# Three gate and shift vectors of a transformer block as column-tiled products on TensorE

## The chip, the cores and the metric

The kernel runs on one core of a Trainium2 chip. The metric is the device time of one execution in microseconds (us), here the median of three runs. Next to it stands one execution that the hardware profiler recorded; the rows of this document come from that one.

## The reference, cut to what matters

One block of a diffusion transformer in fp32, width 2048, with 256 latent tokens `x` and 256 context tokens `ctx`. The vector `c` gives six modulation vectors; what concerns this change is the first line:

```python
mods = jnp.split(jax.nn.silu(c) @ ada_w[l] + ada_b[l], 6, axis=-1)      # ada_w: 2048 x 12288
sh_m, sc_m, gt_m, sh_f, sc_f, gt_f = (m[:, None, :] for m in mods)      # numbers 0 to 5
h_lat = modulate(x_lat, norm_mix_pre[l], sh_m, sc_m)
mix_ctx, mix_lat = token_mixer(h_ctx, h_lat, rows, w_in[l], ...)        # S5, gated delta, mLSTM
x_lat = x_lat + gt_m * rms_norm(mix_lat @ w_out[l], norm_mix_post[l])
f_lat = swiglu(modulate(x_lat, norm_ffn_pre[l], sh_f, sc_f), ffn_w_gate[l], ffn_w_up[l], ffn_w_down[l])
x_lat = x_lat + gt_f * rms_norm(f_lat, norm_ffn_post[l])
```

Modulations 0 and 1 (`sh_m`, `sc_m`) are needed at once, for both token sets. Modulation 2 (`gt_m`) is needed after the mixer, 3 and 4 (`sh_f`, `sc_f`) before the feed-forward layer, 5 (`gt_f`) at the very end. Each is a product of one row of 2048 numbers with a 2048 x 2048 weight block of 16 MB.

## The kernel before

**The big products.** Every large product splits an fp32 weight tile `wf` (512 KB, 1024 columns in each of 128 partitions) into a high part `wh` (ScalarE, `copy`, L168) and a low part `wl = wf - wh` (`tt`, L157, on VectorE or GpSimd), and TensorE adds up three products (`mm3`, tiles `s`). `Unit` is one such tile and `Feed` a list of them that runs through the whole kernel: `Feed.ahead` loads and splits tiles ahead, `Feed.pull(us)` emits so many microseconds of their matmuls. The generators of the stages (`s5`, `gates`, `mlstm`, `prep`, `inv`, `outputs`) yield estimates of time, and `run` pulls as much of the feed between two of their steps. `feed.lo` says which low parts go to GpSimd: 0 none, n each n-th.

**The stages**, with their places in the profiled execution: modulations 0 and 1 as raw tiles `ada` together with the S5 tables (to about 150 us); S5 (150 to 420 us, of it the scan at 217 to 275 us and the part with tables `cf` on GpSimd and products `k` and `y` on TensorE at 276 to 393 us); gates and mLSTM (to 563 us); the gated delta heads (563 to 1010 us, the input weights are used up at 800 us); output product and second norm (to 1072 us); gate and up products (to 1548 us); down product.

**Modulations 2 to 5 in `Modulation`.** A step of `step_` takes one weight tile `vw` of 128 rows by 512 columns (256 KB) and adds it, times one number per partition, to the accumulator `vacc` on VectorE: `ts` (L164) for the first and `stt` (L160) for the other 15 of a block. After 16 steps `finish` sums over the partitions with four matmuls against `ones` (tile `vm`). `Modulation.pull` is called from `Feed.pull`; `rate` sets how many steps are emitted for a microsecond of feed. Modulations 3, 4 and 2 (192 steps) run beside the stages from S5 on, 5 (64 steps) beside the feed-forward products. `load` keeps three tiles in flight.

**What sets the order.** Each engine and each DMA queue works its instructions in order. The order is the emission order as rearranged by the Tile scheduler, which hoists what is ready; nearly all loads stand in one queue, SyncE's (`dma`, L136). `behind(i, first)` adds an ordering without a wait on hardware. In `Modulation.load` the first three loads of modulation 5 are held back by a ScalarE write that needs the last tile of the second norm; those of modulation 3 are not held back at all. The matmuls outside the feed share four PSUM banks `m` (`bank`).

Of the kernel before, what the change touches and what calls it, by code (L numbers as in the profile page):

```python
# [19 lines left out]
P = 128  # L20
# [61 lines left out]
def body(tc, ins, out):  # L82
# [34 lines left out]
    with es:  # L117
# [61 lines left out]
        DVE.memset(mhalf, -0.5)  # L179
        ones = ctile([P, P], "ones")  # L180
# [31 lines left out]
        class Unit:  # L212
# [69 lines left out]
        class Feed:  # L282


            def __init__(self):
                self.units, self.i, self.nl, self.ns = [], 0, 0, 0
                self.gen, self.posts, self.credit, self.done = None, [], 0.0, set()
                self.side, self.open, self.over = None, set(), set()
                self.first, self.lo = {}, 0
# [262 lines left out]

        with pool("st") as st, pool("st2", 2) as st2, pool("aw") as aw, pool("xr") as xr:
# [22 lines left out]
            DVE.memset(csz, 0.0)  # L576
            act(cs32, c32, AF.Tanh, scale=0.5)
# [4 lines left out]
            DVE.tensor_copy(cT.rearrange("p s k -> p (s k)"), ps[:, 0:32])  # L582
            DVE.tensor_copy(csz[:, :, 0:2], cT.rearrange("p s k -> p k s"))
# [205 lines left out]
            def ada_units(b):  # L789
# [4 lines left out]
                for part in range(2):  # L794
                    c0 = (1 - part) * D + b * 512
                    for kp in range(8):
# [8 lines left out]
                        def post(part=part):  # L805
# [18 lines left out]
                            for kk in range(5):  # L824
# [7 lines left out]
                                if kk:  # L832
# [5 lines left out]
                                      aw, 9))  # L838
# [61 lines left out]
        class Modulation:  # L900
# [68 lines left out]

            def move(self, vp):  # L970

                self.end = -(-self.nl // NK) * NK
# [3 lines left out]
        kms, qms, vas = {}, [], []  # L976

        def k_ev(j, ps):
            kms[j] = hold(f"km{j}")
            copy(kms[j], ps)  # L980

        def q_ev(j, ps):
            if j == 0:
                qm = hold("qm")
                qms.extend(qm[:, S * i:S * i + S] for i in range(3))
            act(qms[j], ps, AF.Copy, scale=0.125)

        def v_ev(h0):
            def f(bs):
                for t, ps in bs:  # L990
                    if not vas:
                        vas.append(hold("va")[:, 0:3096].rearrange("p (t h c) -> p t h c", t=4, c=129))
                        DVE.memset(vas[0][:, :, :, P:P + 1], 1.0)
                    copy(vas[0][:, t, h0:h0 + ps.shape[1] // P, 0:P], ps.rearrange("p (h c) -> p h c", c=P))
                    yield
            return f
# [298 lines left out]
        with pool("s1") as s1, pool("s2", 2) as s2:  # L1295
# [3 lines left out]
            feed.lo, side.rate = 2, 0.3  # L1299
# [265 lines left out]
        feed.lo = 3  # L1565
# [297 lines left out]
        feed.lo = 2  # L1863
# [115 lines left out]
        for n in range(4):  # L1979
            gm.append(wo.tile([P, 512], F32, tag="vw" if n < 3 else "vacc", name="gm", bufs=3 if n < 3 else None))  # L1980
# [130 lines left out]
        feed.side = Modulation((5,), 0.12, v2, h2l[15][:, S - 1:S])  # L2111
# [72 lines left out]
```

## Time and profile before

| | before |
|---|---|
| median of three runs | 1808.94 us (1806.25 to 1809.45) |
| the profiled execution | 1800.1 us |
| its span, first to last instruction | 1798.3 us |
| mean granted TensorE clock | 0.949 |
| instructions | 26078 |

The profile gives for each engine its busy time, and for TensorE apart matmuls (PE) and weight loads (PEld). A stretch of the span can be asked for by itself. An fp32 matmul shows as two records (x16 are 8 matmuls); `128*32` behind MATMUL is the part of the array that is used, `128x256` what comes out. PEclk is the granted clock as a share of full speed.

### The profile page before, as it was taken

How to read it: one execution, taken by the hardware profiler on the slowest of the kernel's cores; microseconds unless marked ns; L12 is line 12 of the kernel's file. 1: busy time of each engine (PE TensorE's matmuls, PEld its weight loads, DVE VectorE, ACT ScalarE, POOL GpSimd, SP SyncE). 2: the span in 40 equal slices, each digit the busy share in tenths (PEclk: the TensorE clock that was granted, in tenths of full speed). 3: DMA queues.
4: the chain of work that ended last, by engine and by line, in shares of the span. 5: the costliest groups of instructions: out<-in, count | busy, mean ns of one | idle time of the engine just before them, and what ended most of it. 6: DMA issues, size and time to landing. Idle time of an engine off the chain costs nothing. (4 is left out here: it accounts for less than half of the span.)

```text
span 1798.3 us, 26078 instructions
## 1 busy us (share of the span) xinstructions
PE 1632.5 (91%) x9732; PEld 1331.3 (74%) x9732; DVE 1112.6 (62%) x1793; ACT 756.9 (42%) x1282; POOL 395.7 (22%) x356
## 2 busy tenths in 40 slices
PE   5897997697899889987899979999999999999998
PEld 2555876575687768776677758888888888888886
DVE  3986495748676788765543587657664455444444
ACT  3324212133445236365455474444444444443443
POOL 1005337831213262144553220000000000000001
PEclk9888897798799899998999979999999999999999
DMA  9995133766746746542222459778776666655553
GB/s 328 361 365 120 57 105 98 225 190 201 236 152 210 228 118 196 175 152 71 81 74 95 152 177 332 248 221 281 213 238 188 188 190 192 208 193 194 192 195 132
DMA packets 209525, 340.46 MB, mean 189 GB/s; under 512 B 24837, under 2 KB 68443, under 8 KB 208503
## 3 DMA queue, kind: packets, MB, share of 16 engines
q1 hardware_dynamic: 202535, 330.06, 57.9%
q0 software_dynamic: 1936, 5.60, 1.1%
q10 hardware_dynamic: 4928, 3.15, 0.6%
q8 instruction: 76, 1.25, 0.3%
q14 instruction: 50, 0.41, 0.1%
HBM read 332.11 MB, written 6.64 MB: 188 GB/s over the span
## 5 line engine op out<-in xcount | busy, mean ns | idle before, releaser
L168 ACT ACTIVATE wh<-wf 128x1024 fp32r<-128x1024 f32 (+1 forms) x404 | 420.7, 1044 | 542.2 <-PE s L108 449.0
L157 DVE TENSOR_TENSOR wl<-wf,wh 128x1024 fp32r<-128x1024 f32 (+1 forms) x349 | 423.7, 1218 | 332.4 <-ACT wh L168 331.4
L108 PE MATMUL s<-wl,h2h 128*128 128x512 f32 x704 | 276.4, 393 | 7.7 <-DVE wl L157 7.7
L108 PE MATMUL s<-wh,h2h 128*128 128x512 f32 x704 | 276.0, 393 | 2.9 <-ACT wh L168 2.9
L108 PE MATMUL s<-wh,h2l 128*128 128x512 f32 x704 | 275.8, 392 | 0.2 <-POOL h2l L157 0.2
L160 DVE SCALAR_TENSOR_TENSOR vacc<-vw,cT,vacc 128x512 f32<-128x512 f32 x240 | 203.0, 846 | 78.4 <-DMA vw<-in_ada_w_dram 75.7
L157 POOL TENSOR_TENSOR wl<-wf,wh 128x1024 fp32r<-128x1024 f32 x55 | 136.0, 2474 | 339.3 <-ACT wh L168 298.0
L108 PE MATMUL s<-hh,wh 128*128 128x512 f32 (+1 forms) x448 | 168.1, 387 | 6.7 <-ACT wh L168 3.6
L108 PE MATMUL s<-hh,wl 128*128 128x512 f32 (+1 forms) x448 | 163.4, 371 | 5.5 <-DVE wl L157 5.3
L157 POOL TENSOR_TENSOR rs<-ss,mhalf 128x1 f32<-128x1 f32 x6 | 3.7, 618 | 743.5 <-ACT ps L168 743.5
L108 PE MATMUL s<-hl,wh 128*128 128x512 f32 (+1 forms) x448 | 165.1, 369 | 0.0
L108 PEld LDWEIGHTS s<-wl,h2h 128*128 128x128 f32 x704 | 133.0, 189 | 37.0 <-DVE wl L157 9.7
L108 PEld LDWEIGHTS s<-wh,h2h 128*128 128x128 f32 x704 | 132.9, 189 | 31.1 <-ACT wh L168 3.9
L108 PEld LDWEIGHTS s<-wh,h2l 128*128 128x128 f32 x704 | 133.0, 189 | 28.0 <-POOL h2l L157 0.6
L108 PE MATMUL s<-wh,ah 128*128 128x512 f32 x352 | 136.8, 390 | 0.0
L108 PE MATMUL s<-wh,al 128*128 128x512 f32 x352 | 136.7, 389 | 0.0
L108 PE MATMUL s<-wl,ah 128*128 128x512 f32 x352 | 136.6, 389 | 0.0
L108 PEld LDWEIGHTS s<-hh,wh 128*128 128x128 f32 x448 | 88.5, 198 | 20.2 <-ACT hh L168 4.1
L108 PEld LDWEIGHTS s<-hh,wl 128*128 128x128 f32 x448 | 88.0, 198 | 20.2 <-DVE wl L157 6.3
L108 PE MATMUL s<-wh,mix 128*128 128x512 f32 x256 | 102.6, 428 | 0.1
L108 PEld LDWEIGHTS s<-hl,wh 128*128 128x128 f32 x448 | 88.6, 198 | 14.1 <-issue 3.1
L108 PE MATMUL s<-wl,hh 128*128 128x256 f32 (+1 forms) x256 | 91.3, 358 | 7.0 <-DVE wl L157 6.3
(626 smaller groups left out, 2746.3 us busy)
## 6 DMA issues: line engine op xcount, KB each, us to landing
vw<-in_ada_w_dram SPq DMA_DIRECT2D x256, 256.0 KB
wf<-in_ffn_w_gate_dram SPq DMA_DIRECT2D x96, 512.0 KB
wf<-in_w_in_dram SPq DMA_DIRECT2D x92, 512.0 KB
wf<-in_ffn_w_up_dram SPq DMA_DIRECT2D x88, 512.0 KB
wf<-in_ffn_w_down_dram SPq DMA_DIRECT2D x88, 512.0 KB
wf<-in_ada_w_dram SPq DMA_DIRECT2D x64, 512.0 KB
wf<-in_w_out_dram SPq DMA_DIRECT2D x32, 512.0 KB
x<-in_x_dram SPq DMA_DIRECT2D x4, 1024.0 KB
```

Of the source, the lines that this page charges most:

```text
L108: return cls.queue(nc.tensor.matmul(*a, **k))
L157: return (eng or DVE).tensor_tensor(out=o, in0=a, in1=b, op=op)
L160: return (eng or DVE).scalar_tensor_tensor(out=o, in0=a, scalar=s, in1=b, op0=op0, op1=op1)
L168: return ACT.activation(out=o, in_=a, func=f, **kw)
```

## The change

A class `Products` takes over modulations 3, 4 and 2; `Modulation` keeps 5. A step of `Products` makes 128 output columns: four loads of 512 rows by 128 columns (again 256 KB each, in pieces of 512 bytes instead of 2 KB), and for each load four fp32 matmuls whose stationary operand is 32 columns wide (column 0 holds numbers of `silu(c)`, `cz`) and which go to four 32-partition groups of one bank `vm`. ScalarE copies the bank to `vrow`, and one step later a matmul with `sel4` adds the four rows and turns the result into a column (`vs`). Per modulation that is 16 steps with 64 loads, 256 matmuls of 32 x 128 and 16 of 128 x 1. `pull` takes four units of credit for a step, so that the bytes per microsecond of feed stay as before.

Besides: the first loads of `Products` and of modulation 5 are ordered behind the last weight load of the feed (`feed.last`) in place of the ScalarE write; the ring of the `ada` tiles goes from 9 to 6 buffers, and the first tile of the keys' product (`mk0`) gets buffers of its own and moves ahead of `feed.need("u")`; `feed.lo` becomes 0 at three places. In numbers of instructions: VectorE loses 180 `stt`, 12 `ts` and 12 sums of `vm` and gains 48 sums of 128 x 1 and 14 `wl`; GpSimd loses 14 `wl`; ScalarE gains 48 copies of 128 x 128; TensorE gains 768 matmuls of 32 x 128 and 48 of 128 x 1 and loses 48 of 128 x 1. The number of DMAs stays.

```diff
-                dma(self.wf, self.src)
+                feed.last = dma(self.wf, self.src)
...
+            cz = ctile([P, 56], "cz")
+            DVE.memset(cz, 0.0)
...
+            DVE.tensor_copy(cz[:, 0:NK], cT[:, 0])
...
-                                      aw, 9))
+                                      aw, 6))
...
             feed.add(uu[6:8])
+            mk = stream_fm("mk0", C_MK, 256, 0, 512, k_ev)
+            mk[0].wf_ring, mk[0].wh_ring, mk[0].tag = [xr], [xr], "mk0a"
+            feed.add(mk)
             run(early_tables())
             feed.need("ada3")
-            feed.need("u")
+            feed.need("u", "mk0a")
...
-                    if self.nl < 3 and self.after is not None:
-                        ACT.activation(out=w[:, 0:1], in_=self.after, func=AF.Copy)
                     c0 = i * D + n * 512
-                    dma(w, ada[k * P:(k + 1) * P, c0:c0 + 512])
+                    behind(dma(w, ada[k * P:(k + 1) * P, c0:c0 + 512]), self.after if self.nl < 3 else None)
...
+        class Products:
...
+            def load(self):
+                while self.nl < 4 * self.end and self.nl < self.used + 3:
+                    (i, n), h = self.todo[self.nl // 4], self.nl % 4
+                    w = self.vp.tile([P, 4, P], F32, tag="vw", name="vw", bufs=3)
+                    c0 = i * D + n * P
+                    behind(dma(w, ada[h * 512:h * 512 + 512, c0:c0 + P].rearrange("(k p) c -> p k c", p=P)),
+                           self.after if self.nl < 3 else None)
...
+            def step(self):
+                PE.fed = True
+                self.load()
+                ps = bank("vm")
+                for h in range(4):
+                    self.load()
+                    w = self.w.pop(self.used)
+                    for k in range(4):
+                        PE.matmul(ps[32 * k:32 * k + 32, 0:P], cz[:, 4 * h + k:4 * h + k + 32], w[:, k],
+                                  start=(h == 0), stop=(h == 3))
+                    self.used += 1
+                self.flush()
+                r = self.vp.tile([P, P], F32, tag="vrow", name="vrow", bufs=2)
+                copy(r, ps[:, 0:P])
...
+            def flush(self):
...
+                ps = bank("vs")
+                PE.matmul(ps[:, 0:1], r, sel4, start=True, stop=True)
...
+            def pull(self, us):
+                self.credit += us * self.rate * 2
+                while self.credit > 0 and self.i < self.end:
+                    self.step()
+                    self.credit -= 4.0
...
-        side = feed.side = Modulation((3, 4, 2), 0.15, vp)
-        feed.add(stream_fm("mk0", C_MK, 256, 0, 512, k_ev))
+        side = feed.side = Products((3, 4, 2), 0.15, vp, feed.last)
...
-            feed.lo, side.rate = 2, 0.3
+            feed.lo, side.rate = 0, 0.3
...
-        feed.lo = 3
+        feed.lo = 0
...
-        feed.lo = 2
+        feed.lo = 0
...
-        feed.side = Modulation((5,), 0.12, v2, h2l[15][:, S - 1:S])
+        feed.side = Modulation((5,), 0.12, v2, feed.last)
```

**SyncE's queue in the first stage** (`wf` from `ada_w` are raw tiles of modulations 0 and 1, `wf` from `w_in` weights of the feed, `vw` tiles of modulation 3). Before:

```order
L136 DMA wf<-in_w_in_dram 128x2x512
L136 DMA wf<-in_ada_w_dram 128x2x512
L136 DMA wf<-in_w_in_dram 128x2x512
L136 DMA vw<-in_ada_w_dram 128x512
L136 DMA wf<-in_ada_w_dram 128x2x512
L136 DMA vw<-in_ada_w_dram 128x512 x2
L136 DMA wf<-in_ada_w_dram 128x2x512 x8
L136 DMA wf<-in_w_in_dram 128x2x512
L136 DMA vw<-in_ada_w_dram 128x512
```

And now:

```order
L136 DMA wf<-in_w_in_dram 128x2x512 x2
L136 DMA wf<-in_w_in_dram 128x4x256
L136 DMA wf<-in_ada_w_dram 128x2x512 x6
L136 DMA wf<-in_w_in_dram 128x2x512 x2
L136 DMA wf<-in_ada_w_dram 128x2x512 x18
L136 DMA wf<-in_w_in_dram 128x2x512
L136 DMA wf<-in_ada_w_dram 128x2x512 x5
```

The `vw` loads are gone from this stage; the tile of 128x4x256 is the first of `mk0`, which stood at the stage's end. The first `vw` load now stands behind the last raw tile.

**TensorE in the S5 part with `k` and `y`** (`s` are the feed's products, `k` and `y` those of the S5 tables). Before:

```order
L108 MATMUL s<-wh,hl_575 128x256
L108 MATMUL k<-cf,bz 32x128 x8
L108 MATMUL s<-wh,hh_570 128x256
L108 MATMUL s<-wl,hh_570 128x256
L108 MATMUL s<-wh,hl_576 128x256
```

And now, in the like place:

```order
L108 MATMUL vs<-sel_80,vrow 128x1
L108 MATMUL k<-cf,bz 32x128 x4
L108 MATMUL s<-wh,hh_579 128x256
L108 MATMUL s<-wl,hh_579 128x256
L108 MATMUL s<-wh,hl_584 128x256
L108 MATMUL vm<-vw,cz 32x128 x4
L108 MATMUL k<-cf,bz 32x128 x2
L108 MATMUL vm<-vw,cz 32x128 x4
L108 MATMUL k<-cf,bz 32x128 x2
L108 MATMUL y<-cf,Sc 32x128 x8
```

The groups of four `vm` matmuls, one for each load, stand among the matmuls of the feed and of the stage, and each group waits for the load of its own tile. In the whole program the 768 form 129 unbroken blocks: 79 of one group of four, 18 of two, 21 of three, and 11 others.

**VectorE in the gated delta heads** (`Y` and `Z` belong to the inversion that the heads wait for, `wl` to the feed). Before:

```order
L157 TENSOR_TENSOR Z<-inv,lv_5552 128x512
L160 SCALAR_TENSOR_TENSOR vacc<-vw,cT,vacc 128x512
L157 TENSOR_TENSOR Z<-inv,lv_5552 128x512
L160 SCALAR_TENSOR_TENSOR vacc<-vw,cT,vacc 128x512 x2
L157 TENSOR_TENSOR Y<-inv,lvc 128x256
L157 TENSOR_TENSOR wl<-wf,wh 128x1024
L160 SCALAR_TENSOR_TENSOR vacc<-vw,cT,vacc 128x512
L157 TENSOR_TENSOR Y<-inv,lvc 128x256
```

And now:

```order
L157 TENSOR_TENSOR wl<-wf,wh 128x1024
L157 TENSOR_TENSOR mod_1554<-vs,cols 128x1
L157 TENSOR_TENSOR Y<-inv,lvc 128x256 x3
L157 TENSOR_TENSOR wl<-wf,wh 128x1024
L157 TENSOR_TENSOR Y<-inv,lvc 128x256 x2
L157 TENSOR_TENSOR wl<-wf,wh 128x1024
```

The sums between the steps of the inversion are gone; a small sum of 128x1 for each 128 columns is left.

## Rows read from the trace of the kernel before

**Rows 1.** Page, part 1: busy us, share of the span, instructions.
```profile
PE 1632.5 (91%) x9732; PEld 1331.3 (74%) x9732; DVE 1112.6 (62%) x1793; ACT 756.9 (42%) x1282; POOL 395.7 (22%) x356
```
**Rows 2.** Busy time by stage: stretch, length, then each engine, PEclk, DMA share, GB/s.
```profile
34.00:130.00 96.00, 85.25 (x644) 56.14 (x643) 91.16 (x244) 31.68 (x57) 8.96 (x5) 0.89 1.01 369
276.00:368.00 92.00, 68.90 (x682) 62.12 (x682) 54.74 (x75) 22.20 (x42) 78.97 (x105) 0.80 0.59 176
393.00:563.00 170.00, 150.62 (x762) 122.75 (x761) 117.98 (x205) 78.52 (x165) 34.19 (x23) 0.91 0.65 201
563.00:800.00 237.00, 215.15 (x1546) 181.69 (x1545) 183.62 (x274) 105.78 (x222) 80.47 (x62) 0.96 0.58 177
1072.00:1548.00 476.00, 475.31 (x2146) 393.61 (x2146) 279.78 (x283) 206.42 (x219) 2.00 (x1) 1.00 0.74 229
```
**Rows 3.** The same by stage for instructions with vacc alone (PE, PEld, DVE).
```profile
34.00:130.00 96.00, 0.00 (x0) 0.00 (x0) 11.62 (x16) 0.89 1.01 369
276.00:393.00 117.00, 4.49 (x24) 4.58 (x24) 42.84 (x48) 0.81 0.61 178
393.00:563.00 170.00, 3.05 (x24) 2.99 (x24) 41.86 (x48) 0.91 0.65 201
563.00:800.00 237.00, 5.69 (x40) 5.90 (x40) 68.85 (x80) 0.96 0.58 177
```
**Rows 4.** Loads of vw from 30 to 130 us; DMA issues of the page, part 6.
```profile
L136 SPq DMA_DIRECT2D vw<-in_ada_w_dram x19: 328/341/653, 34.1 to 122.0; - x19
...
vw<-in_ada_w_dram SPq DMA_DIRECT2D x256, 256.0 KB
```
**Rows 5.** TensorE in order of time: start us, us, engine, instruction, records.
```profile
305.14 0.64 PE L108 MATMUL k<-cf,bz 128*32 128x128 f32 x16
305.72 0.39 PE L108 MATMUL s<-wh,hh 128*128 128x256 f32 x1
...
314.42 0.42 PE L108 MATMUL k<-cf,bz 128*32 128x128 f32 x8
314.77 0.38 PE L108 MATMUL s<-wh,hl 128*128 128x256 f32 x1
```
**Rows 6.** TensorE in order of time, one finish of a block in Modulation.
```profile
570.16 0.95 PE L108 MATMUL vm<-ones,vacc 128*128 128x1 f32 x8
570.97 0.49 PE L108 MATMUL s<-hh,wh 128*128 128x512 f32 x1
```
**Rows 7.** GpSimd's groups from 276 to 368 us, and then from 162 to 224 us.
```profile
L157 POOL TENSOR_TENSOR ttmp<-pf,c_im 128x128 f32<-128x128 f32 x44 | 31.8, 750 | 0.7
L157 POOL TENSOR_TENSOR cf<-pf,c_re 128x128 f32<-128x128 f32 x48 | 27.1, 597 | 8.4 <-PE y L108 8.4
L157 POOL TENSOR_TENSOR cf<-cf,ttmp 128x512 f32<-128x512 f32 x12 | 18.7, 1556 | 0.6
...
L157 POOL TENSOR_TENSOR ttmp<-pf,c_im 128x128 f32<-128x128 f32 x20 | 12.8, 670 | 0.4
L157 POOL TENSOR_TENSOR cf<-pf,c_re 128x128 f32<-128x128 f32 x16 | 8.2, 545 | 15.0 <-ACT pf L168 15.0
L157 POOL TENSOR_TENSOR cf<-cf,ttmp 128x512 f32<-128x512 f32 x4 | 5.1, 1286 | 0.3
```
**Rows 8.** Who waited for whom: 276 to 800, 393 to 563, 563 to 800 us.
```profile
DVE vacc L160 <- DMA vw<-in_ada_w_dram: 56.1, 52, 4.9
...
DVE vacc L160 <- DMA vw<-in_ada_w_dram: 15.6, 17, 4.0
...
DVE vacc L160 <- DMA vw<-in_ada_w_dram: 20.4, 17, 2.7
...
PE s L108 <- DVE wl L157: 11.6, 5, 4.2
```
**Rows 9.** Low parts by engine: busy us, mean ns of one.
```profile
L157 DVE TENSOR_TENSOR wl<-wf,wh 128x1024 fp32r<-128x1024 f32 x341 | 422.2, 1241 | 331.8 <-ACT wh L168 331.4
L157 POOL TENSOR_TENSOR wl<-wf,wh 128x1024 fp32r<-128x1024 f32 x55 | 136.0, 2474 | 339.3 <-ACT wh L168 298.0 <-DMA wf<-in_ada_w_dram 31.0 <-PE ada L108 9.6
```

More of the change, by code (lines that the diff above doesn't have):

```diff
@@ L179, in body @@
         DVE.memset(mhalf, -0.5)
+        sel4 = ctile([P, 1], "sel4")
+        DVE.memset(sel4, 0.0)
+        for j in range(4):
+            DVE.memset(sel4[32 * j:32 * j + 1], 1.0)
         ones = ctile([P, P], "ones")
@@ L288, in __init__ @@
                 self.side, self.open, self.over = None, set(), set()
-                self.first, self.lo = {}, 0
+                self.first, self.lo, self.last = {}, 0, None
             def blocked(self):
@@ L551, in early_tables, with k_ev, q_ev, v_ev @@
                     yield 0.9
+        kms, qms, vas = {}, [], []
+        def k_ev(j, ps):
+            kms[j] = hold(f"km{j}")
+            copy(kms[j], ps)
+        def q_ev(j, ps):
+            if j == 0:
+                qm = hold("qm")
+                qms.extend(qm[:, S * i:S * i + S] for i in range(3))
+            act(qms[j], ps, AF.Copy, scale=0.125)
+        def v_ev(h0):
+            def f(bs):
+                for t, ps in bs:
+                    if not vas:
+                        vas.append(hold("va")[:, 0:3096].rearrange("p (t h c) -> p t h c", t=4, c=129))
+                        DVE.memset(vas[0][:, :, :, P:P + 1], 1.0)
+                    copy(vas[0][:, t, h0:h0 + ps.shape[1] // P, 0:P], ps.rearrange("p (h c) -> p h c", c=P))
+                    yield
+            return f
         with pool("st") as st, pool("st2", 2) as st2, pool("aw") as aw, pool("xr") as xr:
@@ L968, in drain, with __init__ @@
                 self.flush()
+        class Products:
+            def __init__(self, mods, rate, vp, after=None):
+                self.after = after
+                self.rate, self.credit, self.vp = rate, 0.0, vp
+                self.todo = [(i, n) for i in mods for n in range(NK)]
+                self.w, self.nl, self.i, self.row, self.used = {}, 0, 0, None, 0
+                self.end = len(self.todo)
+            def load(self):
[5 more added lines that the diff above has]
+                           self.after if self.nl < 3 else None)
+                    self.w[self.nl] = w
+                    self.nl += 1
+            def step(self):
[12 more added lines that the diff above has]
+                copy(r, ps[:, 0:P])
+                self.row = (*self.todo[self.i], r)
+                self.i += 1
+                self.load()
+                PE.fed = False
+            def flush(self):
+                if self.row is None:
+                    return
+                i, n, r = self.row
+                self.row = None
+                ps = bank("vs")
+                PE.matmul(ps[:, 0:1], r, sel4, start=True, stop=True)
+                a = abT[:, (i - 2) * NK + n:(i - 2) * NK + n + 1]
+                tt(mod[i][:, n:n + 1], ps[:, 0:1], a, ALU.add)
+                if i in (2, 5) and n == NK - 1:
+                    tt(mod[i], mod[i], gpost[:, (i // 4) * NK:(i // 4 + 1) * NK], ALU.mult)
+                    ps = bank("vt")
+                    transpose(ps[0:NK, 0:P], mod[i])
+                    r = self.vp.tile([NK, P], F32, tag="vrow", name="grow", bufs=2)
+                    copy(r, ps[0:NK, 0:P])
+                    dma(gtd[i // 4].rearrange("(k p) -> k p", p=P), r)
+            def pull(self, us):
[3 more added lines that the diff above has]
+                    self.credit -= 4.0
+            def drain(self):
+                while self.i < self.end:
+                    self.step()
+                self.flush()
@@ L970, in move @@
             def move(self, vp):
-                self.end = -(-self.nl // NK) * NK
+                self.end = -(-self.nl // 4)
                 self.drain()
                 self.vp, self.end, self.after = vp, len(self.todo), None
[L976 to L996, printed above, removed]
-        side = feed.side = Modulation((3, 4, 2), 0.15, vp)
@@ L1979, in body @@
         for n in range(4):
-            gm.append(wo.tile([P, 512], F32, tag="vw" if n < 3 else "vacc", name="gm", bufs=3 if n < 3 else None))
+            gm.append(wo.tile([P, 512], F32, tag="vw" if n < 3 else "gm3", name="gm", bufs=3 if n < 3 else None))
             dma(gm[n], gtd[0, n * 512:(n + 1) * 512].partition_broadcast(P))
```

## The prediction, made before the change was run

> **What bounds the kernel now.** I read the page first: TensorE is busy 91% of the span, VectorE 62%, GpSimd 22% [rows 1]. A share over the whole span says little here, so I asked for busy time by stage [rows 2]. From 1072 to 1548 us TensorE is busy 475.3 of 476 us at full clock; nothing that VectorE gives up there can shorten it, and the down product behind it looks the same. The change can only act before that, and each stage there has another limit. From 34 to 130 us two things are full at once: VectorE (91.2 of 96 us) and the DMA engines (share 1.01, 369 GB/s). From 276 to 368 us GpSimd is busy 79.0 of 92 us while TensorE runs at a mean clock of 0.80, that is part of the time at the lower of its two levels (1.2 instead of 2.4 GHz). From 393 to 800 us no engine is full: TensorE has 19.4 idle us in the first part (170 less 150.6) and 21.9 in the second (237 less 215.2), VectorE is busy 69% and 77%. Then I asked where the moved work stands [rows 3]: 11.6 us of VectorE in the first stage, 42.8 from 276 to 393, 41.9 from 393 to 563 and 68.9 from 563 to 800 us, together 165.2 us. All of that leaves VectorE.
>
> **The price on TensorE.** The new matmuls have a twin in the kernel: the `k` products, fp32, 32 columns of stationary operand, 128 columns out, four of them side by side in the array [rows 5]. Two groups of four (16 records) hold TensorE for 305.72 - 305.14 = 0.58 us, one group (8 records) for 314.77 - 314.42 = 0.35 us. So a group costs 0.23 us and each unbroken block 0.12 us more for going from the whole array to its strips and back. The change has 192 groups in 129 blocks: 192 x 0.23 + 129 x 0.12 = 44 + 15.5 = 59.6 us, 1.25 us for each of 48 steps. The 48 `vs` matmuls replace 48 `vm` matmuls of the same form; four cost 570.97 - 570.16 = 0.81 us [rows 6], 0.2 each, so that balances, and for standing alone I add nothing (bound: 48 x 0.12 = 6 us). The Trainium skill, "TensorEngine Tiling (Array Packing)", section Tiling Modes, speaks against this change: tiles of the array work in parallel, but changing the tiling mode drains TensorE. The 0.12 us of a block agree with it; the same page's promise of up to four times the throughput, taken without drains, would leave 44 us in place of 59.6. By that estimate, with a third of the difference on the path as in the stages below, the sum would be -15 in place of -10.
>
> By the built order 2 steps stand before the `k` and `y` part, 14 in it, 10 up to the end of mLSTM and 22 in the delta heads before the input weights are used up: 2.5, 17.5, 12.5 and 27.5 us.
>
> **First stage.** 19 `vw` loads stand among the raw tiles [rows 4], 19 x 262 KB = 5.0 MB, which at 369 GB/s [rows 2] are 13.5 us of a full DMA system; the first tile of `mk0` that moves in takes 0.52 MB, 1.4 us. VectorE loses 11.6 us [rows 3] and gains one low part, 1.2 us [rows 9]. Both limits give way by about the same: 12.1 and 10.4 us. Against it stands the ring of 6 in place of 9: three tiles of 512 KB less are 4.3 us of loads less in store when TensorE waits for a table. Between 0 and -12.1 us I take -9.
>
> **The `k` and `y` part.** GpSimd's tables are what this part waits for, and they run slower beside VectorE's sums than in the earlier stretch without them [rows 7]: 750 against 670 ns, 597 against 545, 1556 against 1286. That is 44 x 0.080 + 48 x 0.052 + 12 x 0.270 = 9.3 us. The added 17.5 us of TensorE have cover in 23.1 idle us (92 less 68.9) and in the clock (0.20 x 92 = 18.4 us of full speed lost) [rows 2]. If that cover failed, TensorE would be the limit and the gain gone. Between 0 and -9.3 I take -8; a loss is possible only by waits, which are a rival below.
>
> **Gates and mLSTM.** 12.5 us more on TensorE against 19.4 idle us and a clock of 0.91 (15.3 us of full speed lost) [rows 2]. Some of the idle time goes with the sums: TensorE stood 11.6 us for low parts on VectorE from 276 to 800 us [rows 8]. In the other direction, 14 low parts change from GpSimd (2474 ns) to VectorE (1241 ns) [rows 9], 17.4 us on an engine that has just lost 41.9. I take 0, bounds -10 and +12.5.
>
> **Delta heads to 800 us.** 27.5 us more on TensorE against 21.9 idle us and 9.5 us of lost clock [rows 2], that is 31 us of slack, which no engine can fill wholly because the heads' chain goes back and forth between engines. VectorE falls from 77% to (183.6 - 68.9) / 237 = 48%, so the chain's own steps wait less for it. I take two thirds of the 31 us as cover, 21 us, and so +7; bounds +27.5 (nothing covered) and -12 (the chain gets shorter by half of the idle time besides).
>
> **Costed at nothing.** ScalarE's 48 copies: it is busy 42% [rows 1]; if one is late, the next step's bank is. VectorE's 48 small sums replace 12. Modulation 5's first loads without the ScalarE write, under full TensorE. The loads in 512-byte pieces: the MB are the same, and the DMA share in the stages that take them is 0.58 to 0.65 [rows 2]; no row prices them alone. If every such load took the engines twice its time, 192 x 0.71 us (256 KB at 369 GB/s) more over the 524 us from 276 to 800 us, the share would stay under 0.92, so the engines themselves still have room; the time until a load lands would not be hidden (rival A).
>
> **The sum.** -9 - 8 + 0 + 7 = -10 us: 1790 against the profiled execution's 1800.1 (span 1798.3 and 1.8 around it). That execution is 0.5% under the median of the three runs, 1808.94; I carry the difference over and predict 1799 us. About 0.2%, 3.6 us, is what a measurement of this kernel can tell from no change.
>
> **Rivals.**
> A, slower: TensorE stands at the loads. VectorE stood 56.1 us for `vw` tiles from 276 to 800 us, 15.6 and 20.4 of it in gates, mLSTM and delta heads [rows 8]. There the wait cost little, since VectorE had time. Now the in-order engine that waits is TensorE, with the feed and the heads' products queued behind it, and VectorE and ScalarE behind those. A step needs four loads and has three buffers, so the fourth is issued only when the first group has run, in a queue where weight loads wait for their buffers. If two thirds of those 36 us fall on the path, -10 becomes +14: 1823 us. The point from which it decides is 10 us over the 128 loads of these stages, 0.08 us of standing for each. For it: the same 36 us in the rows. Against it: the order puts feed matmuls between the groups, and part of the standing falls into idle time that is there anyway. Chance 0.27.
> B, much faster: the heads and mLSTM are held up by VectorE, not by TensorE. Then those two stages come at their lower bounds, -10 and -12 instead of 0 and +7: -39 on paper; with three quarters of it, -29, 1780 us. For it: VectorE's 77% beside dependent chains. Against it: of the direct waits of the feed for low parts only 11.6 us show [rows 8]. Chance 0.16.
> C, no change: the change frees what is not the limit. The ring of 6 takes the first stage's gain back and TensorE's 17.5 us that of the `k` and `y` part; -1, -1, 0 and +2 leave 1809 us. For it: VectorE was never waited for long. Against it: two full resources in the first stage. Chance 0.14.
> The forecast itself, -22 to -4 us, has 0.43.
>
> **Numbers.** Faster by over 0.2%: 0.42 of the forecast's 0.43, B's 0.16 and 0.02 of C, 0.60. Within 0.2%: 0.01 and 0.11 and 0.03 from a mild A, 0.15. Slower: 0.24 of A and 0.01 of C, 0.25. The range runs from 1776 (B with most of its bound) to 1827 (A with four fifths of the 36 us); outside lie A with the delta heads uncovered and B's far end, 0.2 together. The forecast's own range is 1787 to 1805.
>
> **What would show it.** In the first stage the last raw tile's product ends some 9 us earlier, with no `vw` load before it; if the DMA share there falls well under 1, the ring of 6 is the reason. GpSimd's `ttmp` from there on take about 670 ns or less. A lone `vm` group holds TensorE for 0.35 us. TensorE's clock rises over 0.80 in the `k` and `y` part. The list of waits shows TensorE at `vw` loads: under 10 us in sum the forecast stands, over 25 us A is right. The feed-forward stages keep their length, to a microsecond or two. The prediction is wrong if the first stage is not shorter, or if the stretch from the last `k` to the first output product grows by more than 15 us.

## The result, and the profile after

The changed kernel takes 1824.02 us, median of 14 runs (1811.57 to 1827.32), the kernel before 1807.51 us in 14 runs beside it: ratio 1.0083, 95% interval 1.0069 to 1.0097. By the ratio it is slower by 15 us (16.5 between the medians). 1799 was predicted, that is a faster kernel, with 1776 to 1827 as the range: the time lies in the range and the direction was wrong. Its profiled execution took 1818.36 us, 18.3 us more than that of before. One profiled execution of the experiments below took 3327 us, nearly twice the others of its kernel, for a reason that its trace does not show; it is not read, and no ratio counts it.

The page of the changed kernel, part 1, as in [rows 1]:

```profile
PE 1690.7 (93%) x11268; PEld 1352.7 (74%) x11268; DVE 971.3 (53%) x1658; ACT 768.7 (42%) x1327; POOL 338.1 (19%) x342
```

VectorE gave up 141 us and GpSimd 58; TensorE took 58 more. The whole reads like a good exchange, and the time rose. The stages, in the columns of [rows 2]:

```profile
34.00:130.00 96.00, 86.32 (x675) 54.94 (x676) 79.93 (x222) 29.41 (x53) 8.91 (x5) 0.85 0.87 304
...
284.00:407.00 123.00, 113.28 (x1311) 89.38 (x1312) 26.48 (x62) 35.17 (x76) 67.36 (x109) 0.91 0.69 192
407.00:815.00 408.00, 395.81 (x3307) 312.60 (x3306) 206.95 (x387) 186.55 (x411) 75.32 (x71) 0.98 0.63 185
...
1090.00:1565.00 475.00, 474.49 (x2144) 393.31 (x2143) 278.72 (x281) 205.48 (x215) 2.40 (x1) 1.00 0.73 226
```

Where TensorE is full, the feed-forward products kept their 475 us (counted from their very first product to the first down product it is 512.6 us, before 509.2). From 407 to 815 us TensorE is busy 97%; VectorE, which the change was to relieve, is down to 51%. GpSimd's tables, as in [rows 7], from 284 to 377 us:

```profile
L157 POOL TENSOR_TENSOR cf<-pf,c_re 128x128 f32<-128x128 f32 x48 | 24.1, 535 | 37.4 <-PE y L108 37.4
L157 POOL TENSOR_TENSOR ttmp<-pf,c_im 128x128 f32<-128x128 f32 x44 | 22.2, 536 | 0.9
L157 POOL TENSOR_TENSOR cf<-cf,ttmp 128x512 f32<-128x512 f32 x12 | 15.3, 1278 | 0.4
```

They are quicker than predicted (`ttmp` 536 ns, before 750, about 670 or less expected), and now they stand 37.4 us for TensorE's `y`, before 8.4. TensorE's clock from 284 to 407 us is 0.91; before it was 0.80 in [rows 2] and 0.82 over the like stretch, 276 to 396 us. The waits of the whole execution (engine, what it would run, what it waits for: us, times, longest), first the engines', then those of SyncE's DMA queue:

```profile
PE ada L108 <- DMA wf<-in_ada_w_dram: 25.0, 15, 9.0
...
ACT vrow L168 <- PE vm L108: 55.3, 29, 6.9
...
PE vm L108 <- DMA vw<-in_ada_w_dram: 13.5, 15, 2.0
```

```profile
SPq L136 <- PE vm L108: 154.6, 83, 6.5
```

And one lone group on TensorE, in order of time as in [rows 5]:

```profile
644.21 0.42 PE L108 MATMUL vm<-vw,cz 128*32 128x128 f32 x8
644.56 0.71 PE L108 MATMUL KK<-yk 128*128 128x128 f32 x4
```

It holds TensorE for 0.35 us, the predicted price to the digit. So the price was right, TensorE's direct waits at `vw` are 13.5 us (between the forecast's 10 and rival A's 25), and still 15 us are lost.

### The profile page after: what moved, and what is told of

The parts are those of the page before. It is cut to its first block, busy times and chain, and to the rows that moved or that the text cites. A ratio compares the mean times of both kernels' runs of the same rounds, so it can differ in the third digit from the quotient of the medians.

```text
span 1816.6 us, 28954 instructions
## 1 busy us (share of the span) xinstructions
PE 1690.7 (93%) x11268; PEld 1352.7 (74%) x11268; DVE 971.3 (53%) x1658; ACT 768.7 (42%) x1327; POOL 338.1 (19%) x342
## 5 line engine op out<-in xcount | busy, mean ns | idle before, releaser
L157 DVE TENSOR_TENSOR wl<-wf,wh 128x1024 fp32r<-128x1024 f32 (+1 forms) x363 | 440.7, 1218 | 396.1 <-ACT wh L168 386.9
L157 POOL TENSOR_TENSOR wl<-wf,wh 128x1024 fp32r<-128x1024 f32 x41 | 100.2, 2446 | 211.7 <-ACT wh L168 181.4
L108 PE MATMUL s<-wh,hl 128*128 128x256 f32 (+1 forms) x256 | 88.7, 348 | 0.0
```

The source lines that it names most:

```text
L108: return cls.queue(nc.tensor.matmul(*a, **k))
L157: return (eng or DVE).tensor_tensor(out=o, in0=a, in1=b, op=op)
```

## The experiments

Each was timed in rounds beside the kernel before, whose median in the four series was 1804.8 to 1806.6 us. The table has the profiled executions, cut where the same instruction starts in all of them: the first `y` product, the first `glu`, the first `oT` (the mLSTM is done), the last `s` of the input weights with `hh` on the left, the end. "Heads" is from the first `oT` to that `s`. One execution is no median: where the code of a stage is the same, the columns differ by up to some 4 us ("behind" 993.4 to 997.6 in the four kernels that have the code of before there).

| kernel | median us | to `y` | `k`/`y` part | gates, mLSTM | heads | behind |
|---|---|---|---|---|---|---|
| before | 1807.5 | 276.5 | 119.6 | 160.6 | 244.0 | 997.6 |
| changed | 1824.0 | 284.5 | 122.6 | 148.3 | 259.2 | 1002.0 |
| first stage of before | 1821.8 | 270.6 | 126.6 | 157.9 | 258.9 | 998.1 |
| ring of 6 alone | 1807.5 | 285.7 | 119.8 | 160.5 | 245.7 | 993.4 |
| changed, loads left out | 1785.2 | 282.9 | 110.0 | 141.1 | 249.1 | 999.2 |
| changed, one group of four | 1791.0 | 286.6 | 122.1 | 139.9 | 244.3 | 998.3 |
| before, loads left out | 1771.0 | 279.7 | 116.0 | 149.8 | 230.8 | 996.7 |
| loads unread | 1846.5 | 292.3 | 143.9 | 152.1 | 251.2 | 1004.3 |
| loads on GpSimd's queue | 1837.6 | 290.0 | 123.2 | 146.5 | 273.3 | 1003.4 |
| half steps | 1821.8 | 284.1 | 130.0 | 152.6 | 254.9 | 1001.4 |
| GpSimd's splits back | 1830.8 | 284.8 | 123.3 | 154.9 | 263.9 | 1001.7 |
| before, VectorE's splits alone | 1780.4 | 278.9 | 122.4 | 156.5 | 227.5 | 994.5 |
| one group of four in the heads | 1809.5 | 288.2 | 125.0 | 148.2 | 244.7 | 1001.9 |
| products for one modulation | 1779.4 | 267.6 | 123.8 | 158.8 | 225.9 | 997.3 |
| no GpSimd splits later | 1781.1 | 276.2 | 121.3 | 156.7 | 227.4 | 997.2 |
| products for two | 1815.2 | 270.6 | 161.4 | 163.3 | 219.6 | 997.9 |

### First stage: taken back, and its ring alone

Ring of nine and `mk0` behind the first stage in the changed kernel:

```diff
-                                      aw, 6))
+                                      aw, 9))
...
-            feed.add(mk)
...
+        feed.add(stream_fm("mk0", C_MK, 256, 0, 512, k_ev))
```

> The changed kernel with its first stage as before: ring of 9 for the ada tiles, and mk0 added behind the first stage with the feed's own buffers. The products on TensorE stay. Theory (the ring of 6 starves the first stage, TensorE's load wait of 25.0 us there against 10.3 before): the last ada product ends 10 us or more earlier than in the changed kernel (146.9 us), since the vw loads stay out of this stage, and the whole time falls by 8 to 14 us, to some 1811. Rival (the first stage is set by the order of the tables, not by the ring): ada ends within 3 us of 146.9 and the time stays within 4 us of the changed kernel.

Measured 1821.76 us, ratio 1.0074 (1.0047 to 1.0100). The first stage is 14 us shorter, the median only 2, which is within the two intervals. The `k`/`y` part takes 4 us more, the gates and the mLSTM 9.6. To see what a stage is filled with, I add up from the timeline how long each matmul holds TensorE: from its start to that of the next one, less the idle time between them. By this the gates' and mLSTM's 9.6 us are 4.6 of the feed (422 matmuls in place of 410, with `mk0` back), 1.8 of one more step of `Products`, and 3.1 of idle time.

In the kernel before, `aw, 6` in place of `aw, 9` alone:

> The kernel before with the ada ring at 6 in place of 9, nothing else. Theory (ring of 6 costs by itself): 4 to 12 us slower than before, all of it before 160 us. Rival (the ring is not what costs): within 3 us of before.

Measured 1807.46 us, ratio 1.0000 (0.9986 to 1.0014). In its profile the first `y` comes 9 us later than in that of before, which is itself 0.4% under its median; over ten runs nothing of it is left. By the medians, then, some microseconds of the first stage, either way, do not reach the end of this kernel. That the stages behind it wait for the weights' products, which go on meanwhile, is a likely reason and not a shown one: the profiled execution with the ring of 6 is 6.8 us longer in all than that of before.

### Loads left out, and three quarters of the products left out

```diff
+                    if len(self.keep) < 3:
                         w = self.vp.tile([P, 4, P], F32, tag="vw", name="vw", bufs=3)
...
+                        self.keep.append(w)
+                    w = self.keep[self.nl % 3]
```

> The changed kernel, with the weight tiles of Products loaded only three times per pool and used again and again: 186 of 192 loads are left out, TensorE's matmuls all stay. Theory that TensorE's added matmuls are the cost of the delta heads: the stretch from the first KK product to the last input product (643 to 814 us, 15 us longer than before) shortens by under 4 us, and the whole by at most 8. Rival (TensorE stands at the loads, forecast's rival A): that stretch shortens by 10 us or more, the whole by 15 or more.

Measured 1785.18 us, ratio 0.9876 (0.9846 to 0.9905): 39 us less than the changed kernel, which looked like rival A.

```diff
-                    for k in range(4):
+                    for k in range(4 if h == 0 else 0):
```

> The changed kernel with all loads of Products, but only the first of four groups of matmuls of each step; three quarters of those sums are left out. TensorE loses 144 groups, some 45 us, and nobody waits for three of four loads. Theory (TensorE's matmuls are the cost): 12 to 25 us faster than the changed kernel, most of it after 643 us. Rival (loads as such, by their traffic in 512-byte pieces and their places in SyncE's queue, slow the feed): under 6 us faster.

Measured 1790.98 us, ratio 0.9897 (0.9866 to 0.9928): 33 us less. Two causes that each seem to hold the whole loss and more call for a control: the kernel before with its loads left out in the same way.

> The kernel before, in which modulations 3, 4 and 2 take only the first three of their loads in each pool and read them again and again; all sums on VectorE stay (the modulations come out different). It is the counterpart of the run with the changed kernel's loads left out (-39 us against the changed kernel, -21 us against the kernel before). Theory 'standing' (a load costs the changed kernel because TensorE's products and SyncE stand for one another): VectorE's sums never made TensorE or the weight loads wait much (36 us of VectorE's waits at vw in the whole program), so this kernel gains little: 1798 to 1806. Theory 'traffic' (the 50 MB cost the weight stream's transfers their share of the engines, whoever reads them): the same 50 MB are gone here, so the gain is of the same size: 1770 to 1785.

Measured 1771.03 us, ratio 0.9799 (0.9780 to 0.9819): 34 us less than the kernel before. The loads cost both kernels about the same, whoever reads them, and without them the changed kernel is still the slower, by 14 us. So they are not what the change lost, and what looked like rival A falls.

### Standing for the loads, in three ways

All loads made into buffers that nobody reads, the products from one fixed tile:

```diff
+                    w = self.vp.tile([P, 4, P], F32, tag="vw", name="vw", bufs=2)
...
-                    self.w[self.nl] = w
+                    self.w[self.nl] = self.fix
```

> The changed kernel with all its loads of modulations 3, 4 and 2 still made, into two buffers that nobody reads; the products read one fixed tile (the modulations come out different). Products and traffic are all there; TensorE no longer waits for a load, nor SyncE for a product. Theory 'standing': as without the loads, 1783 to 1795. Theory 'traffic': as the changed kernel, 1818 to 1828.

Measured 1846.5 us, ratio 1.0220 (1.0172 to 1.0267), slower than either theory. SyncE's waits in it say why it does not decide:

```profile
SPq L136 <- DMA vw<-in_ada_w_dram: 207.4, 167, 4.5
```

With two buffers SyncE stands 207 us for its own transfers (46.7 in the changed kernel), with the weight loads behind it. What it does show: the kernel can be some 22 us slower than the changed one without any wait of TensorE for these loads. That SyncE's standing is the reason is likely; nothing here separates it.

The loads from the gates on issued by GpSimd:

```diff
-                    behind(dma(w, ada[h * 512:h * 512 + 512, c0:c0 + P]...
+                    behind(self.q(w, ada[h * 512:h * 512 + 512, c0:c0 + P]...
...
+            side.q = dma_p
```

> The changed kernel; from the gates on (about 400 us) the loads of the modulations are issued by GpSimd in place of SyncE, so that no weight load stands behind one that waits for a product. TensorE's own waits for these loads stay. If SyncE's standing is what costs: the part that the run without loads gained behind 407 us (some 18 to 26 us) comes back in its larger part, 1800 to 1812. If TensorE's waits at the loads are it: 1818 to 1828, or slower, since GpSimd's own work then stands at the products too. If traffic is it: 1820 to 1828.

Measured 1837.59 us, ratio 1.0171 (1.0154 to 1.0188). The standing went along to the other queue, and the heads became 14 us longer. TensorE stands 11.7 us at `vw` in them, 6.6 in the changed kernel; GpSimd has steps of the heads' chain besides, and what their delay costs is not shown:

```profile
POOL vw L142 <- PE vm L108: 145.7, 44, 9.7
```

Each step cut in two of eight products, so that no load of a burst waits for the burst's own first group:

```diff
-                for h in range(4):
+                for h in (0, 1) if self.part is None else (2, 3):
...
-                    self.credit -= 4.0
+                    self.credit -= 2.0
```

> The changed kernel with each step of 16 products cut in two of 8, at half the interval, the halves added by one more VectorE sum (48 more). Three groups are prefetched, so of four groups in one go the fourth is loaded only once the first has run, and of two in one go both are there. If the burst of four is what makes TensorE and SyncE stand: the waits of TensorE for vw (18 + 17 us) and of SyncE for products (155 us) fall by half or more, and the time to 1806 to 1816. If traffic or the products' own time is it: within 4 us of the changed kernel, 1820 to 1828.

Measured 1821.84 us, ratio 1.0086 (1.0063 to 1.0109): no difference from the changed kernel. TensorE's waits at `vw` did not fall (16.3 us in place of 13.5), and SyncE's standing for `vm` rose from 154.6 us:

```profile
SPq L136 <- PE vm L108: 204.9, 88, 14.2
```

The time is the same with 155 and with 205 us of such standing. A queue that is as far ahead as its buffers allow stands for something most of the time; the sum of these waits is no price here.

### The splits apart from the products

GpSimd's splits back in the changed kernel (`feed.lo` 2, 3 and 2 in place of 0), then the kernel before with 0:

> The changed kernel with one part undone: every second or third weight split from the gates to the first delta heads is GpSimd's again, as in the kernel before; products and loads as changed. If moving the splits to VectorE is a gain of its own (TensorE's waits for a split, 15 us of rows in the kernel before, are gone in the changed one): slower than the changed kernel by 3 to 12 us, 1827 to 1836. If VectorE's splits gave nothing, since TensorE is full there anyway: within 3 us, 1821 to 1827.

> The kernel before with that part alone: no weight split on GpSimd from the gates to the first delta heads; the sums stay on VectorE. If the splits are a gain by themselves: 1795 to 1803. If VectorE, which has the sums as well here (72 to 84% busy in these stages), has no room for them: 1806 to 1815, and the splits could go over only because the sums went.

Measured 1830.78 us, ratio 1.0137 (1.0104 to 1.0169), and 1780.37 us, ratio 0.9868 (0.9840 to 0.9895). **This splits the change in two parts of opposite sign.** Three numbers alone in the kernel before gain 24 us (by the ratio; 15 us below the range of the first theory); the products, with the changed first stage and its 2 us, then lose 39 (2.15%). Beside the products the splits are worth 0.5%, without them 1.3%. In the other order the products and the first stage alone lose 25 us (1.0137), and the splits then give 10 back. So the parts do not add up: a loss of 25 and a gain of 24 would leave 1, and the change stands at 15.

Where the 24 come from, by VectorE's rows from the gates to the end of the heads, first of the kernel before (396 to 801 us):

```profile
L160 DVE SCALAR_TENSOR_TENSOR vacc<-vw,cT,vacc 128x512 f32<-128x512 f32 x120 | 106.0, 884 | 37.4 <-DMA vw<-in_ada_w_dram 36.0
L157 DVE TENSOR_TENSOR wl<-wf,wh 128x1024 fp32r<-128x1024 f32 x44 | 56.5, 1283 | 17.0 <-ACT wh L168 16.8
L160 DVE SCALAR_TENSOR_TENSOR cv<-raw,cw,cv 128x510 f32<-128x510 f32 x20 | 19.0, 965 | 3.5 <-ACT cv L168 3.4
```

then with VectorE's splits alone (401 to 785 us):

```profile
L160 DVE SCALAR_TENSOR_TENSOR vacc<-vw,cT,vacc 128x512 f32<-128x512 f32 x120 | 93.6, 780 | 27.5 <-DMA vw<-in_ada_w_dram 26.6
L157 DVE TENSOR_TENSOR wl<-wf,wh 128x1024 fp32r<-128x1024 f32 x58 | 75.1, 1295 | 20.4 <-ACT wh L168 20.0
L160 DVE SCALAR_TENSOR_TENSOR cv<-raw,cw,cv 128x510 f32<-128x510 f32 x20 | 15.7, 807 | 0.0
```

VectorE takes 14 splits more, 18.6 us, and its 120 sums give 12.4 back, `cv` 3.3: their means are 12 and 16% shorter. The means hide how. The range of the same 120 sums (shortest, median, longest in ns), before and then with VectorE's splits alone:

```profile
L160 DVE SCALAR_TENSOR_TENSOR vacc<-vw,cT,vacc x120: 728/751/2893, 400.0 to 771.4; 128x512 f32<-128x512 f32 x120
```

```profile
L160 DVE SCALAR_TENSOR_TENSOR vacc<-vw,cT,vacc x120: 725/747/1745, 405.9 to 755.5; 128x512 f32<-128x512 f32 x120
```

The median sum is as long as before; a few are longer by a whole instruction of GpSimd. One of them, in order of time (start us, us), a split on GpSimd and the sum that comes on VectorE while it runs:

```profile
611.47 2.85 POOL L157 TENSOR_TENSOR wl<-wf,wh 128x1024 fp32r<-128x1024 f32 x1 [18.83 <-ACT wh L168]
...
612.09 2.77 DVE L160 SCALAR_TENSOR_TENSOR vacc<-vw,cT,vacc 128x512 f32<-128x512 f32 x1
```

The sum ends 0.54 us behind the split, as if it had begun only shortly before the split's end. Of the 120 sums of before, the 94 that met no work of GpSimd took 747 ns in the mean, the 12 that met one of its splits 1847. The Trainium skill, "SBUF — State Buffer", section "SBUF: two separate sides", has a port pair that VectorE and GpSimd lock against each other, for a whole instruction, where VectorE's has two inputs in SBUF and GpSimd's reads it; `vacc` and `cv` are of that kind, and the trace agrees. Over the whole stretch, the stage row of before, then of this kernel:

```profile
396.00:801.00 405.00, 364.48 (x2301) 303.90 (x2302) 301.60 (x479) 182.58 (x386) 113.96 (x84) 0.94 0.61 189
```

```profile
401.00:785.00 384.00, 352.73 (x2290) 293.29 (x2289) 294.61 (x493) 180.20 (x384) 82.77 (x70) 0.97 0.64 197
```

VectorE is busy 7 us less with more splits on it, TensorE idle 9 us less and its clock 0.97 in place of 0.94; 16.5 of the gain lie in the heads, though some 4 us of that are 17 matmuls of the feed that now stand in earlier stages. TensorE's direct waits in this stretch say who had held it: for splits on GpSimd 0.2 us before, for those on VectorE 9.7 and now 10.3, but for VectorE's `Y` and `Dm` of the chains 7.3 and 5.9, now 3.5 and 0.4, and for the sums' `vacc` 4.6, now none.

### Where the products cost

One group of four up to the end of the mLSTM only, then in the heads only (`k in range(4 if self.all or h == 0 else 0)`, with `self.all` changed at the heads' start):

> The changed kernel; up to the end of the mLSTM (555 us) only one of a step's four groups is multiplied (the modulations come out different), in the delta heads all four; all loads stay. Of 39 us of products there (22.9 + 6.9 + 9.4) 29 are left out. With one of four everywhere the kernel gained 33 us. If TensorE's columns cost mostly in the delta heads, where it is 96 to 100% busy: 1814 to 1824. If each stage hands on what it loses: the gain is in proportion, 29 of 53 us of products left out, so about 18 us: 1803 to 1809.

> The counterpart: all four groups up to 555 us, one of four in the delta heads (31 us of products there, 23 left out; the modulations come out different). If the columns cost mostly in the heads: 1793 to 1803. If in proportion: 24 of 53 us left out, about 15 us, 1806 to 1812.

Measured 1803.65 us, ratio 0.9984 (0.9970 to 0.9998), and 1809.5 us, ratio 1.0012 (0.9991 to 1.0034): 20 and 15 us less than the changed kernel. Both lie in the ranges of "in proportion"; that the columns cost mostly in the heads is refuted. The first has no profile that could be read, so where its 20 us come from stays open. In the second the heads are 14.5 us shorter, and TensorE is as full as before; its stage rows, of the changed kernel, of this one, and of the kernel with VectorE's splits alone:

```profile
555.00:815.00 260.00, 252.88 (x2309) 200.75 (x2308) 123.98 (x217) 113.34 (x253) 64.75 (x58) 0.99 0.60 177
```

```profile
561.00:806.00 245.00, 236.16 (x1873) 191.05 (x1872) 126.22 (x217) 111.88 (x253) 64.31 (x58) 0.99 0.62 186
```

```profile
558.00:785.00 227.00, 212.16 (x1562) 179.34 (x1561) 178.92 (x281) 106.38 (x225) 70.43 (x57) 0.98 0.61 187
```

With sums on VectorE, TensorE is busy 212 us in the heads and the heads take 227; with products 253 and 260. The difference of 33 us in time is 41 of work less 8 of idle time. Of the work in the changed kernel, this is the products':

```profile
L108 PE MATMUL vm<-vw,cz 128*32 128x128 f32 x704 | 31.4, 280 | 6.7 <-DMA vw<-in_ada_w_dram 6.6
```

These 31.4 us overlap with other matmuls at their ends; the products hold TensorE for 27.6 us. Another 10.4 us are the feed's: 801 of its matmuls stand in the heads, 771 with VectorE's splits alone, because the gates and the mLSTM, with products among them too, got through fewer (410 in place of 452). So the heads by themselves overstate the loss. Both stages together have nearly the same matmuls of the feed (1211 and 1223) and take 407.5 us against 384.0: 41.3 us of products cost 23.5, and TensorE's idle time falls from 31.2 to 12.2.

Then products for modulation 3 alone, sums for 4 and 2, VectorE's splits, the first stage of before:

```diff
+        side = feed.side = Chain(Products((3,), 0.15, vp, feed.last), Modulation((4, 2), 0.15, vp))
```

> Splits on VectorE and the first stage of the kernel before; modulation 3 (16 steps, to about 400 us) as products, modulations 4 and 2 as VectorE's sums. With no products this stood at 1780 us, with 48 steps of them at 1824 (of which the changed first stage is 2): 0.9 us a step. If every step costs the same wherever it stands: 1791 to 1799. If the k and y part has room on TensorE (86 of 110 us busy in the kernel before) and only the delta heads pay: 1774 to 1785, and this may beat the version without products.

Measured 1779.36 us, ratio 0.9855 (0.9838 to 0.9872): the same as without products. Sixteen steps up to 400 us cost nothing, and they give nothing either. And for modulations 3 and 4, pulled at 1.0, 0.45 and 0.3 in place of 0.7, 0.3 and 0.2:

> As the run with modulation 3 as products, but modulations 3 and 4 (32 steps, pulled faster so that they end by about 555 us), and modulation 2 alone as VectorE's sums in the delta heads. If every step costs 0.9 us: 1805 to 1813. If only the delta heads pay: 1776 to 1788. If the stages before them pay once TensorE's room there is used up: between, 1788 to 1805, and more than twice what the 16 steps cost.

Measured 1815.2 us, ratio 1.0053 (1.0037 to 1.0070). The number is nearest to the first theory, 0.9 us a step, and 2 us over its range; the stages refute an even price. From `glu` to the end of the heads it takes 383 us, without products 384; the `k`/`y` part takes the whole loss. Its stage row and TensorE's waits there, of this kernel, then of the one with 16 steps:

```profile
271.00:432.00 161.00, 132.20 (x1530) 99.92 (x1524) 28.43 (x66) 35.79 (x81) 67.02 (x109) 0.83 0.66 185
```

```profile
PE vm L108 <- DMA vw<-in_ada_w_dram: 27.1, 24, 3.2
```

```profile
268.00:391.00 123.00, 109.73 (x1306) 87.53 (x1300) 28.63 (x67) 32.90 (x74) 66.93 (x109) 0.92 0.71 199
```

```profile
PE vm L108 <- DMA vw<-in_ada_w_dram: 11.4, 11, 2.4
```

Some 20 steps in place of 14 there: 38 us more, of which 15.5 are TensorE standing idle more (its waits at `vw` grew by 15.7), and the clock falls from 0.92 to 0.83. The 9.5 steps behind this part cost nothing visible. Pulled this fast, the products do stand for their loads: rival A's mechanism, at a rate that the change does not use.

### The later splits

The kernel with VectorE's splits alone, and 0 in place of 1 from the output weights on:

```diff
-            feed.lo = 1
+            feed.lo = 0
             ms = []
```

> The kernel before with no weight split on GpSimd from the gates on, and none either in the stages behind, where all of them are GpSimd's (the last delta heads and the output product). If a split on GpSimd (2.47 us and a place in its order, against 1.24 us) holds the weight stream wherever it stands: 1765 to 1777. If VectorE is wanted for other work there: 1780 to 1795.

Measured 1781.05 us, ratio 0.9871 (0.9856 to 0.9887): 27 more splits are off GpSimd (13 in place of 40), and nothing more is gained. That fits a gain which comes where VectorE's sums run beside GpSimd's splits, and not from every split on GpSimd.

## Why the prediction was wrong

Step by step, against the profiled executions in the table:

- **The price on TensorE** (0.35 us a lone group, 1.25 us a step) held: 0.35 in the row above. From 284 to 815 us it is 71.9 us from the start of each block to the next matmul; 6.9 of them are standing at `vw` inside a block and 4.5 idle time behind one, which leaves 60.4 in place of the 57.5 that were counted for 46 steps.
- **First stage, "-9"**: it is 8 us longer. With its order and ring of before, the first `y` came at 270.6 us in place of 276.5, so the loads' leaving was worth some 6. The ring of 6 cost 9 by the profiles (3 had been counted), and the matmuls of the `mk0` tile, of which the sum counted the loading and the low part, lie in it now. But little of what this stage gains or loses reaches the end (14 us shorter gave 2; 9 us longer gave 0).
- **The `k` and `y` part, "-8"**: GpSimd's tables gained 16 us where 9.3 were counted, and TensorE became the limit; 3 us longer. That the gain is gone if TensorE's cover fails was named; the cover was taken to hold.
- **Gates and mLSTM, "I take 0"**: 12.3 us shorter. 35 of the feed's matmuls are gone from them: 16 more stand in the first stage now, 6 in the `k` and `y` part, 13 in the heads.
- **Delta heads, "two thirds of the 31 us as cover, and so +7"**: the heads became 15.2 us longer, and with equal splits (259.2 against 227.5) 32 us, more than the bound of 27.5 that stood for "nothing covered". Part of that is the feed's matmuls from the stage before them, so gates, mLSTM and heads are better read together: with equal splits they lost 23.5 us, where the two terms say 7.
- **"Costed at nothing" and the splits**: 14 splits going from GpSimd to VectorE were weighed in one sentence, for the mLSTM, by their own duration. Alone they are worth 24 us, most of it in the heads. No term of the sum had them.
- **Behind the heads**, no term: 4.4 us longer, by 2.2 up to the first output product and 3.3 between the first gate product and the first down product, less 1.5 between these. The kernels with products in the heads have 998 to 1004 us here, the others 993 to 998; why stays open.

**The step that failed is the cover.** The kernel that the sum priced, with products and without a term for the splits, was run: it is the one with GpSimd's splits back, and it lost 25 us where 10 were to be gained. So the splits hide a part of the error and are not its cause. From the first `y` to the end of the heads its products hold TensorE for 60.5 us, against 57.5 counted, and the sum had all but 7 of these covered by two kinds of slack.

- The first is idle time: 64.8 us of TensorE's in the three stages before, 29.7 in this kernel. It gave 35 us.
- The second is the clock, with 18.4, 15.3 and 9.5 us of "full speed lost". The granted clock did rise, from 0.82 to 0.92, from 0.90 to 0.94 and from 0.96 to 0.98, which by that way of counting is some 24 us of full speed regained. But the matmuls that were there before hold TensorE for 3 us less in all; one of the feed with 512 columns holds it for 253 ns in both kernels. That lost clock was no slack.

So some 38 us of cover stood for 50.5, and the 8 us off for GpSimd's tables went to nothing, since TensorE became the limit there. The three stages came to +17.9 us in place of -1, although 4 us of the feed had moved out of them. The first stage, +8.3 in place of -9 in this kernel, is most of the rest in the profiles; by the medians above, little of that reaches the end.

The same account explains why the parts do not add up. The splits alone already take TensorE's idle time from 40.5 to 31.3 us between 396 and 801 us; what they fill is not there for the products. In the change, the loss of 39 us by the products and the gain of 24 by the splits leave 15. Rival A came out at the right time, 1823, by the wrong mechanism: its 36 us of waits are 13.5, the loads cost the kernel before as much, and TensorE with the products on it is busy 97%. That the measured time lies in the range at all is owed to this rival's place at its slow end, and to the splits.

"The stretch from the last `k` to the first output product grows by more than 15 us" did not come true (465.4 us before, 465.6 now) although the heads lost 15, because 12.3 us went from the gates and the mLSTM and 4.8 from the end of the `k` and `y` part. A mark that spans two stages hides what goes from one to the other.

What else stays open: the 20 us that the changed kernel gains with three quarters of the products left out before the heads. Of the profiles that could be read, none shows more than 8.4 us there (gates and mLSTM, 148.3 against 139.9).

## What to carry to other kernels

Idle time of an engine is one account: when a change has several parts, work out what the first leaves before the second is covered from it, and try the parts apart. A low mean clock of a stretch is slack only if its matmuls take longer there; look at their rows first. The best version here is the smallest part of the change: three numbers in the kernel before, 1780 us, 1.3% faster than before and some 2% faster than the whole change. Before an experiment that leaves something out is read as the cause of a change's loss, the same is to be left out of the kernel before.

## What the runs showed of the hardware that was not expected

- An elementwise step that moves from GpSimd to VectorE can cost VectorE less than its own time: 14 splits of 1.3 us more, and VectorE is busy 7 us less, since its sums fell from 884 to 780 ns in the mean, `cv` from 965 to 807 and smaller rows with them. The sums that met a split on GpSimd took up to 2.9 us. The other way round GpSimd's `ttmp` took 750 ns beside the sums and 536 in the changed kernel, where VectorE is busy 26.5 of 123 us; in the stretch of 670 ns [rows 7] there were no sums, but VectorE was busy 37.2 of 62 us.
- GpSimd's split takes 2.59 us where VectorE's takes 1.28 in the same stretch. The Trainium skill, "GPSIMD Engine Reference", section "Key points", has VectorE about twice as fast for elementwise work; the trace agrees.
- Loading the 192 tiles of 256 KB costs each kernel 34 to 39 us, far more than TensorE's visible waits at them (none before, 13.5 us with the products): without them VectorE's version fell to 1771 us, TensorE's to 1785, at DMA shares that had stood at 0.6. What in the loads costs this is not shown.
- The mean granted clock of a stretch can rise without its matmuls getting shorter: 0.82 to 0.92 in the `k` and `y` part of the kernel with GpSimd's splits back, 0.90 to 0.94 and 0.96 to 0.98 behind it, while a feed matmul of 512 columns held TensorE for 253 ns in the mean in it and in the kernel before (249 in the changed kernel, at 0.91 to 0.99).
